# dt's projection in plain fp32, in four tiles of 32 columns

## The chip, the cores and the metric

The kernel runs on one core of one Trainium2 chip. The metric is device time in microseconds of one execution, as the median of several runs; a profiled execution gives a trace beside its own time. PE (TensorE) multiplies matrices, DVE (VectorE) and ACT (ScalarE) work elementwise and read PE's results from PSUM, POOL (GpSimd) works elementwise on SBUF alone, SP (SyncE) issues the DMAs.

## The reference

Input x has 512 tokens of 1024 features. One Mamba-2 layer and one differential attention layer follow each other, with a shared key/value projection between them and a final norm. The change lies in the first layer, in the part that gives each token and head its step dt and the decays made of it:

```python
h = rms_norm(x, norm_g)
zxbcdt = h @ w_in
z = zxbcdt[..., :SSM_D_INNER]
xbc = zxbcdt[..., SSM_D_INNER:SSM_D_INNER + SSM_CONV_DIM]
dt_raw = zxbcdt[..., SSM_D_INNER + SSM_CONV_DIM:]
...
dt = jax.nn.softplus(dt_raw.astype(jnp.float32) + dt_bias.astype(jnp.float32)).reshape(b, s, G, R)
a = -jnp.exp(a_log.astype(jnp.float32)).reshape(G, R)
y = ssd_chunked_scan(xs * dt[..., None], a * dt, bm, cm)
y = y + d_skip.astype(jnp.float32).reshape(G, R, 1) * xs
y = gated_group_rms_norm(y.reshape(b, s, SSM_D_INNER), z, gate_norm_g).astype(x.dtype)
return x + y @ w_out
```

dt_raw has 32 columns, one per head. In the scan, decays are exponentials of differences of the running sum of a * dt.

## The kernel before

**Split matmuls.** The large products run in a reduced fp32 type (F32R) with both operands split into a high part and a remainder: `mm3` (line 235) issues high x high, high x low, low x high into one accumulator. ACT makes the high part (`whi` of the weights with the norm's gain folded in, `a_hi` of x), DVE the remainder (`wlo`, `a_lo`). Weights come in pieces of 1 MB (`raw`), two buffers each for raw, whi and wlo, so a new piece is split when PE has let go of the piece before the last. x arrives transposed in fp32 as four tiles `xt` of two 128-row blocks each; the row norm's factor is applied to results, as a column per token (`r_col`) or a row over tokens (`r_row`).

**The order.** Nearly all of the first layer is ordered by a scheduler that simulates the engines and lays their queues; each engine then works its queue strictly in turn. `z0`'s projection is written first (accumulators `pz`), then dt, then per group g the projections of B, C and x (`pg`), the convolution (`xc`), and the state-space step `ssd(g)`. `high_priority` moves the weight splits forward.

**Around the change** (lines 380 to 470). After the first half of `z0`, ACT takes the squares of x (`sq`, sums in `ass`), DVE turns them into 1/rms (`y_i`, `y_y`, `y_c`, ending in `ar_col`, the r_col tile), Pool multiplies the identity by it (`adiag`, line 310), one plain fp32 matmul turns that into a row (`aps_r`), and ACT copies it to `ar_row`. dt's weights `dtw_raw` (128x8x32) arrive by a small DMA. For each of the 8 blocks of features ACT writes the high part twice and DVE the remainder twice into `dw`, 128 columns wide: high, high, low, low, of 32 heads each. Sixteen matmuls of 512 columns, `dw` against a_hi and a_lo, fill `ps_dt`, whose 128 partitions then hold the high and the low products. Per chunk c of 128 tokens, ACT copies 32 partitions and DVE adds the other 32 into `pre`, whose partitions are (chunk, head); then comes the factor from `ar_row` and the bias. A softplus by a series (`e`, `q`, `pl`, `dtp`), a cumulative sum (`acs`) and an exponential (`toe`) follow; three transposes (`ps_tt`) bring dtp, acs and toe to token-major (`tok`).

**What depends on it.** `acs` goes to DRAM (`acs_d`) and comes back broadcast as `dec`, one 1 MB transfer per group; Pool subtracts and masks (lines 553 and 554), ACT takes the exponential of `dec`. In `ssd(g)`, PE multiplies C and B (`pcb`), transposes the two halves of x (`pxt_0`, `pxt_1`, which need the SiLU of the convolution, in place on `xc`), builds states (`psA`, `psB`) and the output within the chunk (`pyd`, in two tiles of 64 columns of PE's array).

Of the kernel before, what the change touches and what calls it, by code (L numbers as in the profile page):

```python
# [9 lines left out]
F32 = mybir.dt.float32  # L10
F32R = mybir.dt.float32r
I32 = mybir.dt.int32
AF = mybir.ActivationFunctionType
ALU = mybir.AluOpType
# [3 lines left out]
P = 128  # L18
# [3 lines left out]
KD = D // P  # L22
# [3 lines left out]
H = 32  # L26
NQ = 4
# [11 lines left out]
C_GA, C_GK, C_GB, C_GG, C_SG, C_DTB, C_AL, C_CB, C_CW = 0, 8, 16, 24, 40, 41, 42, 43, 75  # L39
# [24 lines left out]
def trunk(ctx, tc, x, x_t, par, w_dt, w_in, w_out, w_kvqg, w_bo, d_skip, lam_qk, fin_g, out):  # L64
    nc = tc.nc
    V, A, T = (Ordered(tc, e) for e in (nc.vector, nc.scalar, nc.tensor))
# [14 lines left out]
    def ss_bank(name):  # L81
        turns[0] += 1
        tag = "mm" if turns[0] % turns[1] >= 3 else "ss"
        return psum.tile([P, 512], F32, tag=tag, name=name, bufs=3 if tag == "ss" else 4)
# [13 lines left out]
    prm = const.tile([P, C_CB], F32, name="prm")  # L98
# [203 lines left out]
    def scales(tag, ss):  # L302

        V.tensor_scalar(out=ss, in0=ss, scalar1=ROOT2 / D, scalar2=ROOT2 * EPS, op0=ALU.mult, op1=ALU.add)
        col = res.tile([P, NT], F32, tag="r_col", name=f"{tag}r_col")
        V.tensor_copy(col, rsqrt(ss, NT, "y"))
        w = small.tile([P, NT + 1, P], F32, tag="wide", name=f"{tag}diag", bufs=2)
        GP.memset(w[:, NT], 1.0)
        for t in range(NT):
            GP.tensor_tensor(out=w[:, t], in0=ident, in1=col[:, t:t + 1].to_broadcast([P, P]), op=ALU.mult)  # L310
        ps = long_bank(f"{tag}ps_r")
        T.matmul(ps, lhsT=w[:, NT], rhs=w[:, 0:NT].rearrange("p t n -> p (t n)"), start=True, stop=True)
        row = res.tile([P, S], F32, tag="r_row", name=f"{tag}r_row")
        A.copy(row, ps)
        return col, row
# [14 lines left out]
    def new_h(tag):  # L330
        return [res.tile([P, KD, S], F32R, tag=f"hT_{i}", name=f"{tag}_{i}") for i in ("hi", "lo")]
# [9 lines left out]
    hh, hl = new_h("a")  # L341
# [4 lines left out]
    bp2 = bctx.enter_context(tc.tile_pool(name="bp2", bufs=2))  # L346
# [17 lines left out]
    xt = [bp2.tile([P, 2, S], F32, tag="yl", name=f"xt{i}", bufs=4) for i in range(4)]  # L364
# [29 lines left out]
    r_col, r_row = scales("a", ss)  # L394
    V.tensor_scalar(out=sg1, in0=prm[:, C_SG:C_SG + 1], scalar1=0.5 * (1.0 - LAM0), scalar2=None, op0=ALU.mult)
    dtw_raw = sm.tile([P, KD, H], F32, name="dtw_raw")
# [1 line left out]

    dw = bp2.tile([P, KD, 2, 2, H], F32R, tag="yh", name="dw", bufs=4)
    for k in range(KD):
        src = dtw_raw[:, k, :].unsqueeze(1).to_broadcast([P, 2, H])
        gk = prm[:, C_GA + k:C_GA + k + 1]
        A.activation(dw[:, k, :, 0], src, AF.Copy, scale=gk)
        V.scalar_tensor_tensor(out=dw[:, k, :, 1], in0=src, scalar=gk, in1=dw[:, k, :, 0].bitcast(F32), op0=ALU.mult, op1=ALU.subtract)
    ps_dt = ss_bank("ps_dt")
    for k in range(KD):
        w = dw[:, k].rearrange("p a b h -> p (a b h)")
        T.matmul(ps_dt, lhsT=w, rhs=hh[:, k, :], start=k == 0, stop=False)  # L410
        T.matmul(ps_dt, lhsT=w, rhs=hl[:, k, :], start=False, stop=k == KD - 1)

    pre = sm.tile([P, P], F32, name="pre")
    for c in range(NQ):
        sl, hi, lo = (slice(i * H, (i + 1) * H) for i in (c, 0, 1))
        cs = slice(c * P, (c + 1) * P)
        A.copy(pre[sl, :], ps_dt[lo, cs])
        V.tensor_tensor(out=pre[sl, :], in0=ps_dt[hi, cs], in1=pre[sl, :], op=ALU.add)
    for c in range(NQ):
        sl = slice(c * H, (c + 1) * H)  # L420
        V.tensor_tensor(out=pre[sl, :], in0=pre[sl, :], in1=r_row[sl, c * P:(c + 1) * P], op=ALU.mult)
    V.tensor_scalar(out=pre, in0=pre, scalar1=prm[:, C_DTB:C_DTB + 1], scalar2=None, op0=ALU.add)
    e1 = sm.tile([P, P], F32, name="e1")
    A.activation(e1, pre, AF.Abs)
# [240 lines left out]
    hh, hl = new_h("b")  # L665
# [335 lines left out]
    h = DH - 1  # L1001
# [131 lines left out]
```

## Time and profile before

| | us |
|---|---|
| time, median of 3 runs | 729.48 (729.27 to 730.88) |
| the profiled execution, its time | 729.15 |
| the profiled execution, its span | 727.0 |
| PE busy | 713.5 (98%) |
| DVE busy | 528.0 (73%) |
| ACT busy | 433.7 (60%) |
| POOL busy | 117.7 (16%) |

The span is from the first to the last instruction of the trace. A timeline row reads: start, duration, engine, line, operation, tile written <- tiles read, shape, how many, and in brackets the idle time ahead with what ended it. A helper records nearly all operations, so their line is 55 and the tile's name tells them apart. Matmuls are pipelined: one is recorded as longer than the distance to the next, so PE's rate is read from starts. A plain fp32 matmul is recorded as two passes.

### The profile page before, as it was taken

The numbers are of one execution on the slowest core, as the hardware profiler recorded it, in microseconds if no ns is written. First come the engines' busy times: TensorE is split into PE (matmuls) and PEld (weight loads), VectorE is DVE, ScalarE is ACT, GpSimd is POOL, SyncE is SP. The second block draws the span as 40 slices with busy tenths as digits, with TensorE's granted clock in tenths as the row PEclk, the third lists the DMA queues.
The fourth block names the chain that finished last, engine by engine and source line by source line (L and its number), as shares of the span: only waits on it lengthen the run. The fifth ranks groups of instructions, "written<-read, shape, count | busy, mean of one in ns | idle before, by whom it ended". The sixth has DMA issues, their size and how long they took to land.

```text
span 727.0 us, 10819 instructions
## 1 busy us (share of the span) xinstructions
PE 713.5 (98%) x3989; PEld 593.1 (82%) x3989; DVE 528.0 (73%) x1202; ACT 433.7 (60%) x965; POOL 117.7 (16%) x158
## 2 busy tenths in 40 slices
PE   9999999999999999999999999999999999999996
PEld 7787888888888888887788869888988898889874
DVE  4688964979479668569995846657667857785886
ACT  5948573654735527527534348667766756756566
POOL 0108241412315024150110101000000000000002
PEclk9999999999999999999999999999999999999999
DMA  8634313314133231231122310331221131122003
GB/s 302 233 131 162 116 59 117 117 58 175 58 117 116 95 137 60 91 142 59 59 70 105 116 59 9 117 115 59 94 82 58 59 117 59 59 90 85 29 1 115
DMA packets 12916, 70.86 MB, mean 97 GB/s; under 512 B 1728, under 2 KB 2496, under 8 KB 5312
## 3 DMA queue, kind: packets, MB, share of 16 engines
q1 hardware_dynamic: 12576, 69.90, 26.5%
q8 instruction: 31, 0.51, 0.3%
q10 hardware_dynamic: 288, 0.28, 0.1%
q14 instruction: 21, 0.17, 0.1%
HBM read 68.02 MB, written 2.16 MB: 97 GB/s over the span
## 4 chain that ended last, share of the span: by engine, by line
PE 90%; DVE 7%; ACT 1%; issue 1%; POOL 0%; ACTq 0%; DVEq 0%; POOLq 0%
PE pg L55 21%; PE po L55 14%; PE pz L55 12%; PE pt L55 7%; PE pv L55 6%; PE pq L55 6%; PE pk L55 6%; PE pb L55 3%; PE sc L55 3%; PE pyd L55 2%; PE pc L55 2%; DVE wlo L55 2%; DVE xc L55 2%; PE pyt L55 1%; PE pxt L55 1%; PE psA L55 1%
## 5 line engine op out<-in xcount | busy, mean ns | idle before, releaser
L55 DVE SCALAR_TENSOR_TENSOR wlo<-raw,prm,whi 128x512 fp32r<-128x512 f32 (+1 forms) x256 | 150.4, 633 | 52.7 <-ACT whi L55 51.3
L55 ACT ACTIVATE whi<-raw,prm 128x512 fp32r<-128x512 f32 (+1 forms) x256 | 136.8, 606 | 81.4 <-PE pg L55 30.1
L55 PE MATMUL pg<-a_hi,whi 128*128 128x512 f32 x256 | 103.3, 404 | 1.5 <-DVE y_c L55 1.5
L55 PE MATMUL pg<-a_hi,wlo 128*128 128x512 f32 x256 | 102.3, 402 | 0.0
L55 PE MATMUL pg<-a_lo,whi 128*128 128x512 f32 x256 | 102.3, 400 | 0.0
L55 DVE SCALAR_TENSOR_TENSOR xc<-pg,prc,xc 128x511 f32<-128x511 f32 (+2 forms) x96 | 69.6, 738 | 4.8 <-ACT xc L55 4.4
L55 PEld LDWEIGHTS pg<-a_hi,whi 128*128 128x128 f32 x256 | 48.1, 188 | 13.1 <-issue 1.9
L55 PEld LDWEIGHTS pg<-a_hi,wlo 128*128 128x128 f32 x256 | 48.1, 188 | 11.0
L55 PEld LDWEIGHTS pg<-a_lo,whi 128*128 128x128 f32 x256 | 48.1, 188 | 10.7
L55 PE MATMUL po<-whi,yh 128*128 128x512 f32 x128 | 51.4, 402 | 1.5 <-DVE xc L55 0.8
L55 PE MATMUL po<-wlo,yh 128*128 128x512 f32 x128 | 51.1, 399 | 0.0
L55 PE MATMUL po<-whi,yl 128*128 128x512 f32 x128 | 50.4, 398 | 0.0
L55 PE MATMUL pz<-wlo,a_hi 128*128 128x512 f32 x128 | 50.3, 399 | 0.0
L55 PE MATMUL pz<-whi,a_lo 128*128 128x512 f32 x128 | 49.8, 398 | 0.0
L55 PE MATMUL pz<-whi,a_hi 128*128 128x512 f32 x128 | 49.6, 401 | 0.0
L971 POOL TENSOR_TENSOR ot<-ot,fg 128x512 f32<-128x512 f32 x4 | 5.1, 1289 | 256.9 <-ACT ot L55 256.9
L55 ACT ACTIVATE s<-s,mx 128x128 f32<-128x128 f32 (+3 forms) x64 | 35.5, 556 | 9.6 <-DVE mx L55 9.1
L55 ACT ACTIVATE xc<-pg,prc 128x512 f32<-128x512 f32 x32 | 24.6, 773 | 26.6 <-DVE pg L55 26.5
L589 POOL TENSOR_TENSOR xe<-xdt,tok 128x256 f32<-128x256 f32 x24 | 17.3, 749 | 139.6 <-DVE xdt L55 139.6
L55 DVE CUSTOM_DVE_ANT_0 s<-sc,bias 128x128 f32<-128x128 f32 (+3 forms) x64 | 29.4, 488 | 12.2 <-PE sc L55 11.7
L55 ACT ACTIVATE xc<-xc 128x512 f32<-128x512 f32 x32 | 20.0, 629 | 28.3 <-DVE xc L55 28.2
L55 PE MATMUL pv<-whi,b_hi 128*128 128x256 f32 x128 | 36.6, 286 | 0.0
(243 smaller groups left out, 1719.7 us busy)
## 6 DMA issues: line engine op xcount, KB each, us to landing
raw<-in_w_in SPq DMA_DIRECT2D x23, 1024.0 KB, 4.8
raw<-in_w_kvqg SPq DMA_DIRECT2D x16, 1024.0 KB, 4.8
dec<-acs_d SPq DMA_DIRECT2D x8, 1024.0 KB, 4.8
raw<-in_w_out SPq DMA_DIRECT2D x8, 1024.0 KB, 4.8
raw<-in_w_bo SPq DMA_DIRECT2D x4, 1024.0 KB, 4.8
x_tok<-in_x SPq DMA_DIRECT2D x4, 512.0 KB, 9.3
out<-ot SPq DMA_DIRECT2D x7, 256.0 KB, 2.4
raw<-in_w_in SPq DMA_DIRECT2D x4, 256.0 KB, 5.8
```

The lines of the kernel that those rows point to most:

```text
L55: i = op(*args, **kw)
L589: GP.tensor_tensor(out=xe[:, c], in0=xdt[:, c], in1=toe_tok[:, c, hs].unsqueeze(2).to_broadcast([P, R, HD]), op=ALU.mult)
L971: GP.tensor_tensor(out=o, in0=o, in1=f, op=ALU.mult)
```

## The change

The weights of dt are no longer split. DVE multiplies `dtw_raw` by the gain in place, once for all 8 blocks. The matmuls take it and `xt` as they are, in plain fp32: per block k and chunk c one matmul of 32 columns of weights against 128 tokens, into partitions 32c to 32c+31 of `ps_dt`, columns 0 to 127. That is the layout (chunk, head) of `pre`, so the copies and additions go, and the factor from `ar_row` is applied straight out of PSUM.

```diff
-    dw = bp2.tile([P, KD, 2, 2, H], F32R, tag="yh", name="dw", bufs=4)
-    for k in range(KD):
-        src = dtw_raw[:, k, :].unsqueeze(1).to_broadcast([P, 2, H])
-        gk = prm[:, C_GA + k:C_GA + k + 1]
-        A.activation(dw[:, k, :, 0], src, AF.Copy, scale=gk)
-        V.scalar_tensor_tensor(out=dw[:, k, :, 1], in0=src, scalar=gk, in1=dw[:, k, :, 0].bitcast(F32), op0=ALU.mult, op1=ALU.subtract)
+    V.tensor_tensor(out=dtw_raw, in0=dtw_raw, in1=prm[:, C_GA:C_GA + KD].unsqueeze(2).to_broadcast([P, KD, H]), op=ALU.mult)
     ps_dt = ss_bank("ps_dt")
     for k in range(KD):
-        w = dw[:, k].rearrange("p a b h -> p (a b h)")
-        T.matmul(ps_dt, lhsT=w, rhs=hh[:, k, :], start=k == 0, stop=False)
-        T.matmul(ps_dt, lhsT=w, rhs=hl[:, k, :], start=False, stop=k == KD - 1)
-
+        for c in range(NQ):
+            T.matmul(ps_dt[c * H:(c + 1) * H, 0:P], lhsT=dtw_raw[:, k, :], rhs=xt[k // 2][:, k % 2, c * P:(c + 1) * P],
+                     start=k == 0, stop=k == KD - 1)
     pre = sm.tile([P, P], F32, name="pre")
     for c in range(NQ):
-        sl, hi, lo = (slice(i * H, (i + 1) * H) for i in (c, 0, 1))
-        cs = slice(c * P, (c + 1) * P)
-        A.copy(pre[sl, :], ps_dt[lo, cs])
-        V.tensor_tensor(out=pre[sl, :], in0=ps_dt[hi, cs], in1=pre[sl, :], op=ALU.add)
-    for c in range(NQ):
         sl = slice(c * H, (c + 1) * H)
-        V.tensor_tensor(out=pre[sl, :], in0=pre[sl, :], in1=r_row[sl, c * P:(c + 1) * P], op=ALU.mult)
+        V.tensor_tensor(out=pre[sl, :], in0=ps_dt[sl, 0:P], in1=r_row[sl, c * P:(c + 1) * P], op=ALU.mult)
```

The scheduler lays the queues anew, so the order moves beyond these lines, up to the third group; from there on it is the same as before. PE at the end of `z0`, the difference (pz_2 is the accumulator of the third block of tokens; numbers behind it are buffer numbers):

```order
 L55 MATMUL pz_2_139<-whi_217,a_hi 128x512
 L55 MATMUL pz_2_139<-wlo_218,a_hi 128x512
+L55 MATMUL ps_dt<-xt_116,dtw_raw 32x128 x8
+L55 MATMUL ps_dt<-xt_117,dtw_raw 32x128 x8
+L55 MATMUL ps_dt<-xt_118,dtw_raw 32x128 x4
+L55 MATMUL aps_r<-adiag 128x512
+L55 MATMUL ps_dt<-xt_118,dtw_raw 32x128 x4
+L55 MATMUL ps_dt<-xt_119,dtw_raw 32x128 x8
 L55 MATMUL pz_2_139<-whi_217,a_lo 128x512
```

dt's matmuls now stand five pz matmuls earlier than before, and aps_r, which stood two places behind the last of ps_dt with eight pz matmuls behind it, stands inside them, behind 20 of 32; 15 pz matmuls follow the block.

DVE ahead of that, the difference (ass to ar_col is the chain of the row norm's factor, of which the first links are shown):

```order
+L55 TENSOR_TENSOR dtw_raw<-dtw_raw,prm 128x256
 L55 TENSOR_SCALAR ass<-ass 128x4
 L55 TENSOR_SCALAR y_i<-ass 128x4
-L55 SCALAR_TENSOR_TENSOR dw<-dtw_raw,prm,dw 128x2x32
 L55 TENSOR_SCALAR y_y<-y_i 128x4
-L55 SCALAR_TENSOR_TENSOR dw<-dtw_raw,prm,dw 128x2x32
 L55 TENSOR_TENSOR y_c<-y_y,ass 128x4
-L55 SCALAR_TENSOR_TENSOR dw<-dtw_raw,prm,dw 128x2x32
-L55 TENSOR_TENSOR y_c<-y_c,y_y 128x4
-L55 SCALAR_TENSOR_TENSOR dw<-dtw_raw,prm,dw 128x2x32 x2
+L55 TENSOR_TENSOR y_c<-y_c,y_y 128x4
 L55 SCALAR_TENSOR_TENSOR y_c<-y_c 128x4
```

The chain no longer has dw's remainders between its links.

ACT around the decays of groups 0 and 1, before (xc of one tile is the convolution's first product where it reads pg, the SiLU where it reads itself; pg_1, pg_2, pg_3 are C and the two halves of x of group 0):

```order
L55 ACTIVATE whi_558<-raw_556,prm 128x512 x4
L55 ACTIVATE xc_599<-xc_599 128x512
L55 ACTIVATE xc_637<-pg_3_495,prc 128x512
L55 COPY bt_672<-pbt_668 128x384
L55 ACT_TABLE_LOAD
L55 ACTIVATE dec_452<-dec_452 128x2056
L55 ACT_TABLE_LOAD
L55 ACTIVATE xc_618<-xc_618 128x512
L55 ACTIVATE xc_637<-xc_637 128x512
L55 ACT_TABLE_LOAD
L55 ACTIVATE dec_471<-dec_471 128x2056
```

And of the change:

```order
L55 ACT_TABLE_LOAD
L55 ACTIVATE dec_444<-dec_444 128x2056
L55 ACT_TABLE_LOAD
L55 ACTIVATE xc_591<-xc_591 128x512
L55 ACTIVATE xc_629<-pg_3_487,prc 128x512
L55 COPY bt_664<-pbt_660 128x384
L55 ACTIVATE xc_610<-xc_610 128x512
L55 ACT_TABLE_LOAD
L55 ACTIVATE dec_463<-dec_463 128x2056
L55 ACT_TABLE_LOAD
L55 ACTIVATE xc_629<-xc_629 128x512
```

The first dec moved ahead of C's SiLU, and the second ahead of the SiLU of the second half of x, each with a table load before and after. On PE, pxt_0 follows pcb directly, and pxt_1 eight dense matmuls later; from the end of group 0's projections to pxt_1 there are 48 dense matmuls, where there were 39 up to pxt_0 before.

## The prediction

> **What bounds the kernel now.** I read the page's head and its chain first, then the timeline of PE around the projection, then the engines that PE would have to wait for.
>
> ```profile
> span 727.0 us, 10819 instructions
> PE 90%; DVE 7%; ACT 1%; issue 1%; POOL 0%; ACTq 0%; DVEq 0%; POOLq 0%
> ```
>
> PE carries 90% of the chain that ended last, so a microsecond of PE time, or of PE waiting, is a microsecond of the kernel unless a later wait swallows it. PE's timeline around dt's projection (start, duration, engine, line, operation, tile out<-in):
>
> ```profile
> 26.84 0.39 PE L55 MATMUL ps_dt<-a_hi,dw 128*128 128x512 f32 x1
> ...
> 30.34 0.39 PE L55 MATMUL ps_dt<-a_lo,dw 128*128 128x512 f32 x1
> 30.57 0.39 PE L55 MATMUL pz<-whi,a_lo 128*128 128x512 f32 x1
> ...
> 31.04 1.02 PE L55 MATMUL aps_r<-adiag 128*128 128x512 f32 x2
> 31.49 0.79 PE L55 MATMUL pz<-wlo,a_hi 128*128 128x512 f32 x1
> 32.12 0.39 PE L55 MATMUL pz<-whi,a_lo 128*128 128x512 f32 x1
> ...
> 33.74 0.40 PE L55 MATMUL pg<-a_hi,whi 128*128 128x512 f32 x1
> ```
>
> The matmuls overlap, so I go by starts. The 16 of ps_dt take 30.57 - 26.84 = 3.73 us, 0.233 each, as the dense matmuls do, and PE waits for nothing here. aps_r, one plain fp32 matmul, is recorded as two passes and takes 32.12 - 0.233 - 31.04 = 0.85 us, nearly four times a split one of the same shape.
>
> **The change part by part.** *The projection alone.* It becomes 32 plain fp32 matmuls of 128 moving columns into 32 partitions, so 64 passes. No row has such tiles. The nearest are pcb (fp32, 128 columns, whole array) and pyd (fp32, 64 columns, two tiles of the array in turn):
>
> ```profile
> 64.02 1.05 PE L55 MATMUL pcb<-xc,xc 128*128 128x128 f32 x8
> 64.83 0.48 PE L55 MATMUL pg<-a_hi,wlo 128*128 128x512 f32 x1
> 65.15 0.40 PE L55 MATMUL pg<-a_hi,whi 128*128 128x512 f32 x1
> ...
> 78.24 1.01 PEld L55 LDWEIGHTS pyd<-xdt,dec 128*64 128x64 f32 x32 [0.33 <-PE psA L55]
> 78.24 1.15 PE L55 MATMUL pyd<-xdt,dec 128*64 128x64 f32 x32
> 79.33 0.50 PE L55 MATMUL pg<-a_hi,whi 128*128 128x512 f32 x1
> 79.66 0.40 PE L55 MATMUL pg<-a_lo,whi 128*128 128x512 f32 x1
> ```
>
> pcb: (65.15 - 64.02 - 0.233) / 8 = 0.112 us a pass of 128 columns, so 0.056 for 64. pyd: 79.66 - 78.24 - 0.233 = 1.19 us for 32 passes; one after the other they would need 32 x 0.056 = 1.79. So its two tiles run side by side, 16 x 0.056 = 0.90, and some 0.3 goes to entering and leaving the tiled mode. For four tiles the bounds are: one at a time, 64 x 0.112 = 7.17 us; two at a time, 3.58; four, 16 x 0.112 = 1.79. I take four at a time, by the pyd row: its tiles overlap fully, and the code hands out the four tiles in turn. By itself that would save 3.73 - 1.79 = 1.94 us, less 0.3 a visit.
>
> The Trainium skill (TensorE: Matmul & The Clock Gate, "The mechanism" of Part 3) says that a weight load overlaps a running matmul only when their row groups differ; tiles side by side in columns share all rows, and by that rule each pass would wait for its own weights, so the block would cost 7.17 us or more. The pyd rows speak against it: loads busy 1.01 us and matmuls 1.15 us of the same 1.15.
>
> *What PE then waits for.* The order of the changed program splits the block: 20 matmuls, aps_r, 12 matmuls, then 15 pz. It starts five pz earlier than before, at 26.84 - 5 x 0.233 = 25.67. aps_r needs adiag, the last link of a chain from the squares of x:
>
> ```profile
> 23.45 0.17 DVE L55 TENSOR_SCALAR ass<-ass 128x4 f32<-128x4 f32 x1 [3.26 <-ACT sq L55]
> 23.66 0.17 DVE L55 TENSOR_SCALAR y_i<-ass 128x4 int32<-128x4 int32 x1
> ...
> 25.67 0.16 DVE L55 TENSOR_TENSOR y_c<-y_y,ass 128x4 f32<-128x4 f32 x1
> 25.87 0.16 DVE L55 TENSOR_TENSOR y_c<-y_c,y_y 128x4 f32<-128x4 f32 x1
> ...
> 26.26 0.17 DVE L55 COPY ar_col<-y_y 128x4 f32<-128x4 f32 x1
> 26.59 3.34 POOL L310 TENSOR_TENSOR adiag<-ident,ar_col 128x128 f32<-128x128 f32 x4 [3.94 <-DVE ar_col L55]
> ```
>
> Before, adiag is ready at 26.59 + 3.34 = 29.93 and PE comes at 31.04. Now the eight dw operations of DVE between the links are gone; at 0.20 a link (25.67 to 25.87) ar_col starts at 23.66 + 9 x 0.20 = 25.46, Pool 0.33 later, and adiag is ready at 29.13. ACT's squares still set the start. The one new DVE operation, on 128x256, lies in the 3.26 us in which DVE idles ahead of ass; were w_dt late, ass would wait behind it. So:
> - 20 matmuls, 40 passes in fours: 25.67 + 10 x 0.112 + 0.3 = 27.1;
> - PE idles until 29.2, **2.1 us**;
> - aps_r, 0.85: 30.05;
> - 12 matmuls: 6 x 0.112 + 0.3: 31.0;
> - 15 pz at 0.233: pg begins at **34.5, not 33.74: 0.8 late**.
>
> The 1.94 us saved, less 0.6 for two visits, are more than spent in front of aps_r.
>
> *ACT and DVE.* Eight dw activations and eight dw subtractions go, four copies and four additions out of ps_dt too. None is on the chain around 30 us, where PE runs without a gap; the cover is PE's own dense work. They count only through adiag, above, and through the scan that follows.
>
> *The second place: the first group's decays.* The scan (pre, e, q, pl, acs) comes earlier, and the order puts its consumers earlier: on ACT both exponentials of dec now stand ahead of the last SiLU of group 0, which pxt_1 on PE needs. Before, PE waited here for pxt_0:
>
> ```profile
> 66.55 0.40 PE L55 MATMUL pg<-a_hi,whi 128*128 128x512 f32 x1
> 67.55 0.66 PE L55 MATMUL pxt<-ident,xc 128*128 128x128 f32 x4 [0.61 <-ACT xc L55]
> ...
> 56.43 2.56 ACT L55 ACTIVATE whi<-raw,prm 128x512 fp32r<-128x512 f32 x4
> 58.90 0.62 ACT L55 ACTIVATE xc<-xc 128x512 f32<-128x512 f32 x1
> 59.42 0.76 ACT L55 ACTIVATE xc<-pg,prc 128x512 f32<-128x512 f32 x1
> 60.09 0.46 ACT L55 COPY bt<-pbt 128x384 f32<-128x384 f32 x1
> 60.57 1.28 ACT L55 ACT_TABLE_LOAD   x1
> 63.64 1.92 ACT L55 ACTIVATE dec<-dec 128x2056 f32<-128x2056 f32 x1 [1.79 <-POOL dec L554]
> 65.57 1.28 ACT L55 ACT_TABLE_LOAD   x1
> 66.87 1.15 ACT L55 ACTIVATE xc<-xc 128x512 f32<-128x512 f32 x2
> ```
>
> That wait is 67.55 - 66.55 - 0.233 = 0.77 us and goes. In its place: ACT splits the next weights (whi) when PE has let the buffer go, now 0.8 later, at 57.2. From there, in the new order, four splits 2.47, table 1.28, dec 1.92, table 1.28, a SiLU 0.52, the convolution's first product 0.67, bt 0.47, a SiLU 0.55, table, dec, table (4.48), the last SiLU 0.57: 14.2 us, done at 71.4. PE gets to pxt_1 sooner: from the same point it has 48 dense matmuls (11.2), pbt, pcb and pxt_0 (0.33 + 0.90 + 0.44), 12.9 us, so it stands there at 70.1 and waits **1.3 us**. This holds if Pool is done with both dec in time:
>
> ```profile
> 39.95 0.23 DVE L55 TENSOR_SCALAR q<-e 128x128 f32<-128x128 f32 x1 [1.68 <-ACT e L55]
> 45.44 0.42 DVE L55 TENSOR_TENSOR_SCAN acs<-ones,adt 128x128 f32<-128x128 f32 x1
> ...
> 61.27 2.33 POOL L554 TENSOR_SCALAR_AFFINE_SELECT dec<-dec 128x512 f32<-128x512 f32 x3
> ...
> 67.60 2.40 POOL L554 TENSOR_SCALAR_AFFINE_SELECT dec<-dec 128x512 f32<-128x512 f32 x4
> ...
> L55 DVE SCALAR_TENSOR_TENSOR wlo<-raw,prm,whi 128x512 fp32r<-128x512 f32 (+1 forms) x256 | 150.4, 633 | 52.7 <-ACT whi L55 51.3
> ```
>
> Pool ended at 63.60 and 70.00; ACT now asks at 60.9 and 67.6, 2.7 and 2.4 earlier. The scan is to end about 2.3 earlier (estimate: pz_2's last matmul at 31.9, then two zs, e, a table load of 1.28 and e again on ACT, so q near 34.9 instead of 39.95; but the four wlo of the next weights, at the page's 633 ns, now stand inside the 5.9 us from q to acs). The transfers between acs and dec are issued by SP behind the same weight load as before; that load waits for the last of these wlo, near 40, well ahead of the scan's end, so they move with the scan. So add 0.4: a wait of 1.7, a net loss of 1.7 - 0.77 = **0.95 us**. Ends: 0 wait (net -0.77) and 3 us (net +2.2), were the scan no earlier at all.
>
> **Sum.** 0.8 + 0.95 = +1.75 us. The profiled execution took 729.15 us (span 727.0 and 2.15 around it): 730.9. The median of the runs shown is 729.48, 0.33 above it, so I forecast **731.2**.
>
> **The rivals.**
> - *One tile at a time.* 20 matmuls take 20 x 2 x 0.112 = 4.48: 30.45 with the entry, so adiag has long been ready; aps_r until 31.3, 12 matmuls 2.69 + 0.3, pg at 37.8: +4.05, and with the second place +5.0: 734.5. For it: nobody here has run four tiles with four different moving operands; against it, the pyd rows. The skill's rule above is this case. Chance 0.14.
> - *Two at a time.* The wait for adiag shrinks to 1.0, the second visit takes 1.64, pg at 35.2: +1.45 and 0.95: 731.9. pyd shows two tiles, no more. Chance 0.13.
> - *Not slower: the loss falls into a later wait.* The page has such a wait:
>
> ```profile
> L55 PE MATMUL pg<-a_hi,whi 128*128 128x512 f32 x256 | 103.3, 404 | 1.5 <-DVE y_c L55 1.5
> 315.05 0.69 DVE L55 TENSOR_TENSOR dx<-pyd,dx 128x512 f32<-128x512 f32 x1 [3.42 <-PE pyd L55]
> ```
>
> PE waits 1.5 us for one chain of DVE's (y_c). If that chain keeps its time when PE comes 1.75 later, the wait swallows 1.5: 729.7. It decides whether the chain hangs on PE; the second row, some 10 us ahead of it, says it does, since DVE itself waited for PE there. Chance 0.13.
> - *Not slower: ACT has the SiLU in time.* If ACT is 1.3 us quicker than my sum, the second place gives -0.77 and the total is 0.0: 729.5. ACT's rows are steady, but a 0.8 wait did stand there in another order. Chance 0.16. Both of these together would be faster, 728.0: 0.04.
> - That the change does not do what it says is excluded by the order: 32 tiles for 16, and no dw.
>
> **Numbers.** The forecast has 0.40, its own spread about 0.7 either way from the second place. A measurement of this kernel can tell about 0.2% (1.46 us) from no change. Slower by more than that: 0.65 of the forecast's 0.40, and both first rivals: 0.53. Faster: 0.04. Within: 0.43. The range leaves out one tile at a time and the double gain, 0.18 together: 729.0 to 733.0; forecast alone: 730.5 to 731.9.
>
> **What would show it.** Four tiles: matmuls of ps_dt in the new timeline starting in fours, 0.112 apart, the block's own time near 1.8 us. The first wait: idle time of PE ahead of aps_r, put down to Pool's adiag, near 2 us; none there means one tile at a time. pg's first matmul at 34.5. The second: idle ahead of pxt_1 for ACT's xc, and none ahead of pxt_0. After 200 us the two traces should run in parallel; if the y_c wait is shorter by the loss, the third case holds. I am wrong from the start if adiag is ready before 28 us.

## The result, and the profile after

The changed kernel takes 734.75 us (median of 10 runs, 732.47 to 737.49), the kernel before 729.63 us beside it (10 runs, 728.56 to 730.88): a ratio of 1.0075, 95% interval 1.0059 to 1.0091. It is some 5 us slower, where the prediction had 1.7. (Each ratio below is to the kernel before in the same batch of runs; times of different batches are less comparable. Two executions far outside the rest, of 2677 and 4022 us, are left out of medians and ratios.) The profiled execution of the changed kernel happens to be its fastest, 732.47 us; its span is 3.7 us longer than that of before.

The page's head and its chain, for the changed kernel:

```profile
span 730.7 us, 10893 instructions
...
PE 81%; DVE 9%; DMA 3%; ACT 3%; issue 2%; POOL 1%; SPq 1%; ACTq 0%; DVEq 0%; POOLq 0%
```

PE had 90% of the chain and has 81%: the end is now handed on more often by DVE, by transfers and by ACT. There are 74 more instructions; PE has 96 more (64 passes with 64 weight loads, where 16 and 16 stood), and ACT and DVE fewer. The 96 will matter.

PE's timeline at the two places of the prediction (start, duration, operation, what ended the idle time ahead of it):

```profile
26.11 1.30 PE L55 MATMUL ps_dt<-xt,dtw_raw 128*32 128x128 f32 x40
28.04 1.13 PE L55 MATMUL aps_r<-adiag 128*128 128x512 f32 x2 [0.63 <-POOL adiag L310]
29.10 0.86 PE L55 MATMUL ps_dt<-xt,dtw_raw 128*32 128x128 f32 x24
33.48 0.40 PE L55 MATMUL pg<-a_hi,whi 128*128 128x512 f32 x1
...
68.83 0.39 PE L55 MATMUL pg<-a_lo,whi 128*128 128x512 f32 x1
71.05 0.66 PE L55 MATMUL pxt<-ident,xc 128*128 128x128 f32 x4 [1.83 <-ACT xc L55]
```

The 40 passes of the first row start within 1.03 us (26.11 to 27.14, in fours 0.109 apart), so four tiles do run at once. PE then waits less for adiag than forecast, and pg begins at 33.48, ahead of before (33.74). The wait ahead of pxt_1 is there: 71.05 - 68.83 - 0.233 = 1.99 us. So far the loss is 0.95 us at 200 us of the trace (matmul for matmul, counted from the end of both). The rest lies where the prediction expected the traces to run in parallel. All waits of PE in the changed kernel, total, times, longest:

```profile
PE pg L55 <- DVE y_c L55: 2.3, 1, 2.3
PE po L55 <- DVE x_tok L55: 1.9, 1, 1.9
PE pxt L55 <- ACT xc L55: 1.8, 1, 1.8
...
PE aps_r L55 <- POOL adiag L310: 0.6, 1, 0.6
```

The second row is new:

```profile
233.16 0.40 PE L55 MATMUL po<-whi,yl 128*128 128x512 f32 x1
235.41 0.50 PE L55 MATMUL po<-whi,yh 128*128 128x512 f32 x1 [1.85 <-DVE x_tok L55]
```

PE loses 2.06 us here, because DVE's addition of a finished block to x_tok, which frees the PSUM bank, is late. Near 331 us the known wait for y_c has grown by 0.68. Then 0.95 + 2.06 + 0.68 = 3.69 is the whole difference of the two spans. The first question was what the projection has to do with a PSUM bank 200 us later.

DVE and POOL there, first in the changed kernel:

```profile
226.38 0.41 DVE L55 TENSOR_TENSOR dx<-dx,zs 128x256 f32<-128x256 f32 x1
226.72 1.53 DVE L55 SCALAR_TENSOR_TENSOR wlo<-raw,prm,whi 128x512 fp32r<-128x512 f32 x1
228.18 1.27 DVE L55 TENSOR_TENSOR dx<-dx,zs 128x256 f32<-128x256 f32 x1
229.37 2.99 DVE L55 SCALAR_TENSOR_TENSOR wlo<-raw,prm,whi 128x512 fp32r<-128x512 f32 x2
232.28 2.47 DVE L55 TENSOR_TENSOR dec<-dec,pcb 128x512 f32<-128x512 f32 x4
234.68 0.68 DVE L55 TENSOR_TENSOR x_tok<-po,x_tok 128x512 f32<-128x512 f32 x1
```

```profile
226.25 0.26 POOL L541 COPY dec<-dec 128x8 f32<-128x8 f32 x1 [0.74 <-DMA dec<-acs_d]
226.59 5.22 POOL L543 TENSOR_TENSOR dec<-dec,tok 128x512 f32<-128x512 f32 x4
```

then in the kernel before:

```profile
226.77 1.40 DVE L55 SCALAR_TENSOR_TENSOR wlo<-raw,prm,whi 128x512 fp32r<-128x512 f32 x2
228.10 2.47 DVE L55 TENSOR_TENSOR dec<-dec,pcb 128x512 f32<-128x512 f32 x4
230.49 0.68 DVE L55 TENSOR_TENSOR x_tok<-po,x_tok 128x512 f32<-128x512 f32 x1
```

```profile
227.20 0.36 POOL L551 COPY dec<-dec 128x8 f32<-128x8 f32 x1 [2.63 <-DMA dec<-acs_d]
227.65 4.47 POOL L553 TENSOR_TENSOR dec<-dec,tok 128x512 f32<-128x512 f32 x4
```

Both engines run the same operations in the same order. But in the changed kernel POOL's four subtractions begin 1.06 us earlier, while DVE, which follows PE, is later. Three wlo and a dx now fall beside POOL; each wlo takes 1.5 us in place of 0.70, the dx 1.27 in place of 0.41, and x_tok comes at 234.68 in place of 230.49.

POOL is earlier although the transfer that it waits for is issued later. SP's rows, before (first) and changed (second):

```profile
220.52 0.33 SPq L549 DMA_DIRECT2D dec<-acs_d  x1
```

```profile
221.46 0.33 SPq L539 DMA_DIRECT2D dec<-acs_d  x1
```

From issue to POOL's first use it is 6.68 us before and 4.79 after, for the same megabyte. The DMA view of before, from 224.9 to 226.1 us, when this transfer should have been done (queue, packets, MB, share of 16 engines):

```profile
q8 instruction: 1, 0.02, 5.0%
q1 hardware_dynamic: 1, 0.00, 0.1%
```

Two packets are left. One is a piece of 16,384 bytes on the queue called instruction; it starts at 225.07. The other is the last of the 16 completion marks of the decay transfer (packets of 4 bytes at its end), at 226.02; the other 15 had come by 224.87. In the changed kernel the pieces on q8 come at 217.83 and 242.33, none near. There are 31 such pieces before and 32 after, for 8,060 and 8,156 PE instructions in the trace: about 256 to a piece. By their number they are PE's program, and the change made that program 96 instructions longer ahead of this place. The lone mark starts where the piece ends: 225.07 + 0.96 = 226.03. The Trainium skill (Runtime: NRT & Kernel Launch, Instruction fetch mechanics) says the same of the pieces, 256 instructions in 16 KiB, brought by a DMA queue of the engine's own, and calls the cost mostly hidden. No wait of PE is put down to a fetch in these traces; a transfer that meets a piece can pay.

### The profile page after: what moved, and what is told of

It is laid out like the page before. It is cut to its first block, busy times and chain, and to the rows that moved or that the text cites. A ratio compares the mean times of both kernels' runs of the same rounds, so it can differ in the third digit from the quotient of the medians.

```text
span 730.7 us, 10893 instructions
## 1 busy us (share of the span) xinstructions
PE 712.2 (97%) x4037; PEld 590.6 (81%) x4037; DVE 529.7 (72%) x1191; ACT 433.2 (59%) x955; POOL 116.9 (16%) x158
## 4 chain that ended last, share of the span: by engine, by line
PE 81%; DVE 9%; DMA 3%; ACT 3%; issue 2%; POOL 1%; SPq 1%; ACTq 0%; DVEq 0%; POOLq 0%
PE pg L55 18%; PE po L55 13%; PE pz L55 9%; PE pt L55 7%; PE pq L55 6%; PE pv L55 6%; PE pk L55 6%; PE pb L55 3%; DVE wlo L55 3%; PE sc L55 3%; PE pyd L55 2%; PE pc L55 2%; DMA raw<-in_w_in 2%; DVE xc L55 1%; DMA xt<-in_x_t 1%
## 5 line engine op out<-in xcount | busy, mean ns | idle before, releaser
L55 DVE SCALAR_TENSOR_TENSOR wlo<-raw,prm,whi 128x512 fp32r<-128x512 f32 (+1 forms) x256 | 156.0, 655 | 48.7 <-ACT whi L55 47.2
L543 POOL TENSOR_TENSOR dec<-dec,tok 128x512 f32<-128x512 f32 x32 | 36.9, 1181 | 0.6
```

Of the source, the lines that this page charges most:

```text
L55: i = op(*args, **kw)
L543: GP.tensor_tensor(out=dec[:, h], in0=dec[:, h], in1=acs_tok[:, :, R * g + h].unsqueeze(2).to_broadcast([P, NQ, P]), op=ALU.subtract)
```

## The experiments

Three theories stood at first: the new order (with POOL and DVE in each other's way later), chance, and a cost of the tiles themselves. The trace of the first four runs gave the fetch theory its form: **where the pieces of PE's program fall decides how long the decay transfers take, that decides when POOL starts, and that decides how slow DVE is.**

**The changed kernel again.** No edit.

> The changed kernel once more, for a second profile. Theory 1 (new order: the loss is the wait ahead of pxt_1, made larger later on by DVE and Pool working at the same time): median 734 to 736; PE again idles about 2 us ahead of pxt_1 near 71 us, and again about 2 us ahead of po near 233 us for DVE's x_tok. Theory 2 (the later waits are chance: any shift of a microsecond moves them): the wait ahead of pxt_1 stands, those near 233 and 331 us are gone or elsewhere, the median is the same. Theory 3 (the fp32 tiles lower the granted clock): this profile shows a slice before 720 us with PEclk under 1.0, and its matmuls start more than 0.233 us apart there.

734.52 us, ratio 1.0055 (1.0038 to 1.0072). The wait ahead of pxt_1 (2.1 us) and that for x_tok (2.0) are both there again, so the latter is no chance. This profile is 2.1 us longer than the first. Part of it is in its stretches (the stretch, its length, busy time and instructions of PE, PEld, DVE, ACT and POOL, then the granted clock, the DMA share and GB/s):

```profile
234.00:236.00 2.00, 0.36 (x2) 0.00 (x0) 2.00 (x4) 0.56 (x1) 1.41 (x3) 1.00 0.84 262
236.00:238.00 2.00, 1.80 (x5) 1.41 (x6) 2.00 (x5) 1.36 (x1) 0.00 (x0) 0.62 0.62 262
238.00:240.00 2.00, 2.00 (x7) 1.57 (x6) 1.70 (x6) 0.47 (x1) 0.00 (x0) 0.53 0.00 0
240.00:242.00 2.00, 2.00 (x10) 1.63 (x9) 1.08 (x4) 1.99 (x4) 0.00 (x0) 1.00 0.00 0
```

Right behind the 2 us of idling the clock is halved for 3.41 us; matmuls start 0.427 apart in place of 0.233, and the wait has cost 1.5 us more.

**The tiles alone.** The dw splits are put back as work that nothing reads.

```
+    dw = bp2.tile([P, KD, 2, 2, H], F32R, tag="yh", name="dw", bufs=4)
+    for k in range(KD):
+        ...
+        A.activation(dw[:, k, :, 0], src, AF.Copy, scale=gk)
+        V.scalar_tensor_tensor(out=dw[:, k, :, 1], ...)
     V.tensor_tensor(out=dtw_raw, in0=dtw_raw, ...)
```

> The four fp32 tiles alone: the eight dw activations and eight dw subtractions are put back as work that nothing reads, so that ACT and DVE are as busy as before ahead of adiag. The order that results has aps_r ahead of all 64 passes of ps_dt, and at the first group's decays ACT has both last SiLUs ahead of the second dec exponential, as before the change. Theory 1 (new order): no wait of 2 us ahead of pxt_1, the block saves 3.73 - 1.79 - 0.3 = 1.6 us, so 727.5 to 730. Theory 2 (chance): the early gain is the same, but a later wait of 1 to 2 us may eat it: 728 to 732. Theory 3 (the tiles themselves cost, by the clock): 734 or more, as with the whole change.

731.96 us, ratio 1.0018 (1.0003 to 1.0033). No wait ahead of pxt_1, none of the loss of the second place; the x_tok wait of 2.0 us stands. New order explains the first, nothing yet the second. The tiles themselves don't cost what the third theory had (734 or more).

**The other half alone.**

```
     for k in range(KD):
-        A.activation(...); V.scalar_tensor_tensor(...)
+    for i in range(4):
+        V.tensor_tensor(out=dw[:, :, i // 2, i % 2], in0=dtw_raw, in1=<gain>, op=ALU.mult)
```

> The other half alone: PE's 16 dense matmuls of ps_dt and the additions that form pre stay as before, but dw is written by four DVE multiplications in place of eight activations and eight subtractions (the low half of the weights is left out of the computation, and the high half is counted twice). PE's order is that of before, row for row. Theory 1 (new order): no loss, 728.5 to 730.5. Theory 2 (chance): also about 729.6, but with up to 2 us more if the shift of adiag by under a microsecond is enough to move a later wait. A fourth theory, that taking work off ACT and DVE is what costs: 733 or more.

This kernel leaves out the low half of dt's weights and counts the high half twice. 730.42 us, ratio 1.0003 (0.9987 to 1.0018): no change, and no wait for x_tok. Taking this work off ACT and DVE costs nothing that shows.

**One tile at a time.**

```
-    for k in range(KD):
-        for c in range(NQ):
+    for c in range(NQ):
+        for k in range(KD):
```

> The changed kernel with the loops of the projection exchanged: all eight k of one tile, then the next tile, so that neighbouring passes go to the same tile. Every other engine's order is that of the changed kernel. If passes overlap only between different tiles: 64 x 0.112 = 7.2 us of PE in place of 1.8, less the 0.9 us that PE waits ahead of aps_r: PE reaches pg about 4.5 us later, and with theory 1 the median is 738 to 740. If tiles did not matter: the same time as the changed kernel. Theory 2 (chance): the early loss is 4.5 but the sum at the end is anywhere from 1 to 7.

738.02 us, ratio 1.0102 (1.0080 to 1.0124), 3.5 above the changed kernel of the same batch. PE in this run:

```profile
26.00 2.84 PE L55 MATMUL ps_dt<-xt,dtw_raw 128*32 128x128 f32 x28
28.77 1.13 PE L55 MATMUL aps_r<-adiag 128*128 128x512 f32 x2
29.82 3.29 PE L55 MATMUL ps_dt<-xt,dtw_raw 128*32 128x128 f32 x36
...
36.63 0.40 PE L55 MATMUL pg<-a_hi,whi 128*128 128x512 f32 x1
```

28 passes take 2.77 us, 0.099 each: within a tile they start 0.109 apart, and only where one tile gives way to the next do some overlap. pg begins 3.15 us later than in the changed kernel. The x_tok wait is 1.9 us here too, although PE comes 4 us later: it does not depend on how late PE is.

**96 more instructions for PE, and nothing else.** The kernel before; 10 warm-up transposes give way to 29 small matmuls.

```
-    for i in range(24):
+    for i in range(29):
+        T.matmul(warm[i % 4 * H:(i % 4 + 1) * H, 0:64], lhsT=ident[:, 0:H], rhs=ident[:, 0:64], ...)
+    for i in range(14):
         T.transpose(warm[:, 0:P], ident, ident)
```

> The kernel before, with 10 of its 24 warm-up transposes replaced by 29 small matmuls, so that PE's program holds 96 more instructions ahead of everything else, as many as the change adds; the order on ACT, DVE, POOL and SP is that of before, row for row. Fetch theory (PE's program comes by DMA in pieces of 256 instructions; where a piece is fetched while a decay transfer lands, the transfer takes about 2 us more, and in the changed kernel the sixth transfer has lost that collision): the decay transfer issued near 220 us takes 4.2 to 4.9 us to Pool's first use in place of 6.7, those near 131 and 175 us take 5.5 to 7.4, PE waits 2.0 us near 233 us for DVE's x_tok, and the median is 731.5 to 733.5. Lag theory (the wait near 233 comes because PE and DVE are 0.7 us or more late there): no such wait, the median 729 to 731.

733.67 us, ratio 1.0048 (1.0031 to 1.0064). Without any of the change, 3.1 us are lost. POOL and DVE of this run:

```profile
226.48 0.47 POOL L553 COPY dec<-dec 128x8 f32<-128x8 f32 x1 [0.87 <-DMA dec<-acs_d]
227.03 5.55 POOL L555 TENSOR_TENSOR dec<-dec,tok 128x512 f32<-128x512 f32 x4
```

```profile
227.48 1.27 DVE L55 TENSOR_TENSOR dx<-dx,zs 128x256 f32<-128x256 f32 x1
228.67 2.99 DVE L55 SCALAR_TENSOR_TENSOR wlo<-raw,prm,whi 128x512 fp32r<-128x512 f32 x2
```

The sixth transfer takes 4.92 us in place of 6.7, two wlo and a dx are slow, and PE waits 1.2 us for x_tok (2.0 were expected; one wlo fewer is hit) and 2.5 for y_c, behind which the clock is halved. Of the 4.58 us that its profile is longer, 1.04 come in the first 200 us, of which I can't say what is the new warm-up, 1.3 at x_tok and 2.3 at y_c and behind it.

**The changed kernel with 160 more**, 256 with its own 96; **the tiles alone with the same**. The edit is as above, 47 matmuls of 16 columns for 14 transposes.

> The changed kernel, with 14 of the 24 warm-up transposes replaced by 47 small matmuls, so that PE's program holds 160 more instructions ahead of everything else; with the 96 of the change that is 256, one whole piece, and the fetches fall in the program where they fell before. The order on all other engines is that of the changed kernel. Fetch theory: the decay transfer near 221 us takes 6.5 us or more, the wait of 2.0 us near 233 us is gone, and the median is 731 to 732.8. Lag theory: the wait stands, 734 to 735.5.

734.84 us, ratio 1.0055 (1.0034 to 1.0076): missed. The piece comes 3.97 us after the issue and delays nothing, so the transfer takes 4.72 and the wait stands. Besides, aps_r waits 2.3 us in this profile, and the clock is halved behind it.

> The four tiles alone (as in the run with the splits put back), with the same 160 instructions more in PE's program. Fetch theory: the wait near 233 us is gone, and what the tiles save early stays: 728 to 730, against 731.96 without the shift. Lag theory: 731 to 733.

730.69 us, ratio 0.9991 (0.9972 to 1.0009). The same piece at 3.45 us does delay the transfer (5.75 us). What is left of PE's wait for x_tok:

```profile
PE po L55 <- DVE x_tok L55: 0.2, 1, 0.2
```

**POOL's subtractions for group 5 left out.**

```
+                if g != 5:
                     GP.tensor_tensor(out=dec[:, h], in0=dec[:, h], in1=acs_tok[...], op=ALU.subtract)
```

> The changed kernel without Pool's four subtractions for the decays of group 5, the ones that run near 227 to 232 us (so these decays are wrong in the output). All orders are otherwise those of the changed kernel. If these subtractions slow DVE (contention): the two wlo and the dx near 228 to 232 us take their usual 0.74 and 0.41 us in place of 1.5 and 1.27, the wait near 233 us shrinks from 2.0 to under 0.5 us, and the median is 732 to 733. If DVE is slow there for another reason: the wait stands and the median is 734 to 735.5.

731.81 us, ratio 1.0017 (1.0001 to 1.0033). The x_tok wait shrinks to 0.2 us. DVE:

```profile
227.94 0.85 DVE L55 TENSOR_TENSOR dx<-dx,zs 128x256 f32<-128x256 f32 x1
228.72 2.15 DVE L55 SCALAR_TENSOR_TENSOR wlo<-raw,prm,whi 128x512 fp32r<-128x512 f32 x2
```

2.15 in place of 2.99: POOL's subtractions are what slows DVE; not back to 1.40, since POOL's selection, with one tensor to read, now stands beside it.

**The changed kernel with 192 more**, to put the piece where 12 of 14 transfers had been late.

> The changed kernel with 192 more PE instructions in the warm-up (55 small matmuls for 14 transposes), all other orders as in the changed kernel. In the run with 160 more, a piece of PE's program was fetched 3.97 us after the sixth decay transfer was issued and did not delay it; 32 instructions more bring that fetch some 3.7 us earlier, to 0 to 0.5 us after the issue, where 12 of the 14 transfers seen so far were late. Fetch theory: the sixth transfer takes 5.4 to 7 us from issue to Pool's first use, the wait of 2.0 us near 233 us shrinks to under 1.3 us, and the median is 731.5 to 734. If the fetch does not matter: transfer 4.7, wait 2.0, 734 to 735.5.

734.26 us, ratio 1.0043 (1.0025 to 1.0061). The piece came 0.64 us after the issue; the transfer took 5.10 (under the 5.4 expected), and the wait 1.1 us in place of 2.0. Direction as expected, size half; but no lone mark was late (the last came 0.06 us behind the one before it), so that the piece did this isn't shown.

**The last SiLU of group 0 first**, alone and with the 192.

```
+        A.on = ft == 1          # hold the marked operations in the order of the code
         A.activation(xc, xc, AF.Silu)
+        A.on = False
...
         until(f"g{g}")
+        if g == 0:              # the second dec exponential, moved here
+            A.on = True
+            A.activation(decs[1][2], decs[1][2], AF.Exp)
+            A.on = False
```

> The changed kernel with ACT made to issue the last SiLU of group 0 ahead of the second dec exponential, as before the change; PE's program is as long as the changed kernel's. New-order theory: the wait of 2.0 us ahead of pxt_1 shrinks to under 0.8 us, the wait near 233 us stands (its cause is the fetch), median 732.5 to 734, that is 1.2 to 2 less than the changed kernel. If the early wait is paid back later in any case: 734 to 735.5.

733.23 us, ratio 1.0025 (1.0007 to 1.0043), 1.5 below the changed kernel of another batch (734.75; ratio 1.0075, and 1.0055 when run again): the wait ahead of pxt_1 is gone, that for x_tok (1.9) stands. The second place is worth about what the prediction said, or somewhat more.

> Both edits together: the last SiLU of group 0 first, and 192 more PE instructions in the warm-up. If the two causes add up: 1.2 to 2 us below the shifted kernel of this batch, 729.5 to 732, about the time before the change. If they do not: 732 or more.

732.24 us, ratio 1.0018 (1.0001 to 1.0036): 2.0 below the shifted kernel of the same batch, so the two add up, though not quite down to the 732 expected.

**The kernel before again.**

> The kernel before once more, for a second profile. Fetch theory: a piece of PE's program is again fetched near 225 us and the sixth decay transfer again takes over 6 us from issue to Pool's first use, with no wait for x_tok near 233 us; the time is 728.5 to 732. If the late transfer of the first profile was chance: it takes 4.2 to 5 us here, and PE waits for x_tok.

729.79 us. The transfer took 6.57 us, its last mark 1.07 us after the other 15, the piece at 4.40; no wait for x_tok, though PE stands 0.70 us later at 233 us than in the first profile.

All profiles but the one without subtractions in one table (pieces and issues from the DMA records, in us; the wait as the view of waits gives it):

| kernel | PE instructions more than before | piece of PE's program, after the sixth decay transfer's issue | issue to POOL's first use | PE's wait for x_tok |
|---|---|---|---|---|
| before; again; other half | 0 | 4.55; 4.40; 4.70 | 6.68; 6.57; 6.85 | none |
| tiles alone, 256 | 256 | 3.45 | 5.75 | 0.2 |
| changed, 192 more | 288 | 0.64 | 5.10 | 1.1 |
| SiLU first, 192 more | 288 | 0.34 | 4.93 | 1.1 |
| before, 96 more | 96 | -3.6 | 4.92 | 1.1 |
| changed; again; tiles alone; one tile; SiLU first | 96 | -3.4 to -3.6 | 4.79; 4.68; 4.35; 4.68; 4.70 | 1.8 to 1.9 |
| changed, 160 more | 256 | 3.97 | 4.72 | 1.8 |

The wait goes with the transfer's time, row by row, and not with how late PE is (0.7 us late in the second profile of before and in the tiles alone: none and 1.8). Nor does the issue move against PE: it comes 11.69 to 11.71 us ahead of the same matmul, the last before the place of the wait, in all 14 profiles. In the four in which the lone mark is late (before, again, other half, tiles alone with 256), one packet of the transfer starts within 0.02 us of the piece's end, and no other within 0.3 us. In the two rows with 288 no mark is late, and "before, 96 more" has as short a wait without a piece: of the step from 1.8 to 1.1 us the piece is not shown to be the cause. Over the third and the fifth to eighth decay transfers of all 14 profiles (the first two go together, the fourth shares its time with a weight load in most), one completion mark came over 0.4 us after the rest in 20 of the 35 that a piece met between issue and first use, and in 1 of the 35 that none met; there a piece had begun 0.17 us ahead of the issue.

## Why the prediction was wrong

**Four tiles at a time: right.** 40 passes in 1.03 us; with one tile at a time 28 take 2.77. The Trainium skill's rule of the prediction (TensorE: Matmul & The Clock Gate, "The mechanism" of Part 3), by which loads that share all rows would not overlap, is not borne out by these rows.

**The wait ahead of aps_r: right in kind, its size varies.** The prediction took POOL's 3.34 us for adiag from before; in the profiled run it was shorter, as the first row shows, while in the run with SiLU first, of the same code up to there, it was not:

```profile
26.51 1.47 POOL L310 TENSOR_TENSOR adiag<-ident,ar_col 128x128 f32<-128x128 f32 x4 [3.12 <-DVE ar_col L55]
```

```profile
26.17 2.87 POOL L310 TENSOR_TENSOR adiag<-ident,ar_col 128x128 f32<-128x128 f32 x4 [3.14 <-DVE ar_col L55]
```

In the latter DVE runs four wlo beside it from 26.42; in the former these begin at 27.88, since ACT waits for the weights. So PE waits between 0.6 and 2.0 us there (up to 2.7 with the longer warm-up), and the term of +0.8 was -0.26 in the profiled run.

**The second place: right.** A wait of 1.99 us ahead of pxt_1 (1.7 forecast), none ahead of pxt_0; 1.2 us net in the profile (0.95 forecast), and 1.5 between the medians of two batches when it is undone.

**"After 200 us the two traces should run in parallel": this step failed.** The rivals allowed only for a later wait that swallows some of the loss. In its place came one that adds 2.06 us: of the 3.69 us that the profiles differ by, 0.95 are there at 200 us, where the prediction had all of its 1.75. The prediction counted the 96 new PE instructions as time on PE and left out that they move every later fetch of PE's program. Before, such a fetch kept the sixth decay transfer, and with it POOL, out of DVE's way for 1.9 us; the shift took this away. Shown: 96 instructions more in the kernel before bring the wait in (1.2 us of the 3.1 that they cost in all), POOL's subtractions are what DVE loses to, and the wait goes with the transfer's time. The 0.68 us more for y_c has the same look (three wlo in 4.44 us beside POOL's subtractions), but no run isolates it, and where the pieces fall is not enough to tell it: PE waits 1.9 us for y_c in the other half, with before's fetches, and 1.5 in SiLU first, with the changed kernel's.

**The runs above the profiled one.** 3.7 us separate the profiles' spans, 5.1 the medians. The changed kernel's profiled run is the fastest of its ten, 2.3 us under their median; that of before is 0.5 under. In 9 places of the 14 profiles PE's clock was halved for 3.41 us, each time at the end of a wait of PE of 1.8 us or more or within 1.1 us behind it, at about 1.5 us apiece; 22 waits are that long, and the other 13 passed without. The two profiles of before have no such wait, each of the changed kernel three, so the changed kernel might be hit more often. The mean granted clock of each run doesn't show it: 0.9966 and 0.9963 in the two batches of the changed kernel, 0.9965, 0.9973 and 0.9968 for the kernel before in the three later ones. And of the changed kernel's ten runs the three at 0.999, where one such stretch has no room (it would take off 0.0023), took 732.47, 734.02 and 734.63 us, the four at 0.994 and 0.995 734.76 to 737.49: the clock makes a part of the spread, and some 2 us are there without it.

Open: why a piece 3.4 to 4.7 us after the issue delayed only 4 of 14 transfers (the records don't say which of the 16 DMA engines carries it), what the medians have beyond the profiles, and how much of the tiles' early gain could be kept. No version beat both kernels; the tiles alone with 256 more, at 0.9991 (0.9972 to 1.0009), come out even with before.

## What to carry to other kernels

An edit that changes how many instructions an engine has (here PE) moves its later program fetches, and a transfer that meets one can land 1 to 2 us later: compare the time from issue to first use of the same transfers in both traces before explaining a far wait by the edit itself. Where two engines read SBUF beside each other, ask of a transfer that lands *earlier* what it will now collide with. To tell such an effect from the edit, give the old kernel the same number of instructions in a place that costs little, and see what that place costs by itself.

## What the runs showed of the hardware

- Four tiles of 32 columns with all 128 rows run at once: four fp32 passes of 128 columns, with four weight loads, every 0.109 us; on one tile, one pass every 0.109.
- A program fetch of 16 KB can hold back one of the 16 completion marks of a 1 MB transfer: the sixth took 5.75 to 6.85 us to its first use in the four profiles where it did, 4.35 to 5.10 in the others.
- DVE and POOL slow each other where both read only SBUF: wlo 0.70 to 1.5 us, dx 0.41 to 1.27, POOL's four subtractions 4.47 to 5.22. DVE's dec, which reads PSUM (pcb), kept its 2.47 us for four beside POOL's subtractions (before). The records read like turns: beside POOL's subtractions, which end at 227.71, 229.17, 230.35 and 231.81, DVE's wlo, dx, wlo and wlo end 0.55, 0.28, 0.56 and 0.55 us behind one each; and a wlo that ran already when the first subtraction began (227.44, before) kept its 0.74 us, where that subtraction took 1.44 in place of 1.05.
- Behind an idle stretch of about 2 us PE's clock was halved in 9 places of the 14 profiles (of 22 such waits), for 3.41 us each time. The Trainium skill (TensorE: Matmul & The Clock Gate, Part 1) has a free-running window of that length and an idle window as the condition; the length agrees, but here 1.8 to 2.7 us of idling were enough in some runs and not in others.
